# A decoder block on one core: the MLP's hidden-side S sums formed in the up projection, and the down projection's weight operands handled in units of 128x2048

## The chip, the cores and the metric

The kernel runs on one core of a Trainium2 chip. The metric is the device time of one execution in microseconds. The kernel before takes 1153.55 us in the median of three runs (1149.79, 1153.55 and 1154.32). Engines are named as in the profile: PE (TensorE matmul), PEld (its weight load), DVE (VectorE), ACT (ScalarE), POOL (GpSimd), and SP (SyncE, which only issues transfers). A line number Lnnn is one of the kernel before, unless the changed kernel is named.

## The reference

One layer of a decoder on 1024 tokens of 1024 channels (16 meta tokens are put in front and dropped again at the end). All data are float32.

```python
hn = rms_norm(h, norm_mix_w);  proj = hn @ w_in          # 3088 columns
mixed = concatenate([gla_branch(...), short_conv_branch(...)]) @ w_out
h = h + mixed
hn = rms_norm(h, norm_mlp_w)
h = h + square(relu(hn @ w_up)) @ w_down                 # 1024 -> 4096 -> 1024
out = rms_norm(h, norm_final_w)[:, N_META:]
```

The change touches only the last product pair, `square(relu(hn @ w_up)) @ w_down`. The three norm weights, w_up, w_down and the rest are inputs and may not be prepared outside the kernel.

## The kernel before

**Stages.** The first 390 us or so hold the input projection, the linear attention and the convolution. Then follow the output projection (tiles `mo`, `wo`), the up projection (16 groups of 256 hidden channels) and the down projection (four chunks of 1024 hidden channels, that is four groups each).

**Precision.** Each float32 operand is split into a high part, rounded to PE's float32r format by ACT (`split`, L76), and a low part, the difference, formed by DVE (L36). A product is three matmuls: high by high, high by low, low by high (`mm3`, L680 to L682).

**Seven products for eight.** From the up projection on, every product is a 2 x 2 block product in Winograd's form. With A the stationary side and B the moving one:

```
S1 = A21+A22, S2 = S1-A11, S3 = A11-A21, S4 = A12-S2
T1 = B12-B11, T2 = B22-T1, T3 = B22-B12, T4 = B21-T2
```

The seven products are called 1 (A11 B11), 2 (A12 B21), 5 (S1 T1), 6 (S2 T2), 7 (S3 T3), 3 (S4 B22) and 4 (A22 T4). Each has its own operands, and each of these is split.

**The up projection.** A is w_up, B the normalised input. A group's seven products are 12 matmuls each. POOL forms the four S sums of a group (tiles `S`, 128x512), ACT and DVE split the seven operands (`wh_u`, `wl_u`) about a group ahead of PE. `up_first` does products 1 and 2, the loop of phase 3 the other five. ACT takes the accumulators out of PSUM (L746, L886, L911), DVE and POOL add them up (L669), DVE squares the relu (L739), and SP stores four tiles a group (`put`, L740): the blocks of the hidden activation, token half by channel half. Two loads of w_up (`up_load`, L691, 512 KB each) stand among the stores in SP's queue. Their buffers are three, so a load also waits for operands to be split.

**The down projection.** A is the hidden activation, B is w_down. A product is 48 matmuls: four token tiles t, each with 12 matmuls into one PSUM bank. `a_load` (L937) and `b_load` (L943) fetch blocks of 128x2048 (1 MB) into rings of five slots a side, called `A...l` and `B...h` after the buffers that they reuse. `prep` makes the operands of a chunk's products in the order 1 2 5 6 7 3 4. POOL forms S1 to S4 (`each`, 16 operations of 128x512 a chunk), DVE forms T1 to T4 (also 16). `emit` splits A by token tile into pairs (`wh_d`, `wl_d`; eight pairs, so two products' worth) and B by row tile into a unit (`bo<chunk><product>h` and `l`, 128x2048; two units, so product n+1 reuses the unit of product n-1). After each token tile DVE adds the bank to the residual stream h (L669: `h<-da` for products 1, 6, 7, 4; `h<-db` for 2, 5, 3). Banks: four for `da`, four for `db`. At the end h is normalised and stored (L1004 to L1014).

**What sets the order.** Each engine executes its own list in order. A scheduler makes the lists from the order of the source when the program is built. The operands of a product are emitted ahead of the matmuls of the product before it (`ahead = next(st)`).

Of the kernel before, what the change touches and what calls it, by code (L numbers as in the profile page):

```python
# [30 lines left out]
def block_kernel(ctx: ExitStack, tc, x, meta, nmix, w_in, wgu, bgate, gnorm, conv_w,  # L31
# [42 lines left out]
    def split(src, hl, eng=None):  # L74
        """hi and lo parts of a float32 view into float32r views"""
        hi = nc.scalar.copy(hl[0], src)  # L76
        return hi, sub(eng or nc.vector, hl[1], src, hl[0].bitcast(F32))
# [40 lines left out]
    # ------------------------------------------------------------------ phase 1  # L118
    with ExitStack() as p1:
# [165 lines left out]
        with ExitStack() as p1b:  # L285
# [153 lines left out]
            def gla():  # L439
# [195 lines left out]
            # ---- output gate; the two groups' outputs, split, as units (half, group)  # L635
# [83 lines left out]
    def up_ready(g, ps):  # L719
        """operands ps of group g"""  # L720
# [13 lines left out]
    banks = {}  # L734

    def put(g, z, i, h):
        """squared relu of a tile of hidden channels, to DRAM"""
        c, k0 = divmod(2 * g, 8)
        nc.vector.scalar_tensor_tensor(z, z, 0.0, z, op0=ALU.max, op1=ALU.mult)  # L739
        nc.sync.dma_start(hidD[c][:, h * 4:(h + 1) * 4, k0 + i, :], z.rearrange("p (t c) -> p t c", c=P))  # L740

    def up_first(g, e1):
        """the products that need only the first half of the tokens"""
# [5 lines left out]
        put(g, e1, 0, 0)  # L749

    raws = {}
    with tc.tile_pool(name="p2", bufs=1, reuse_waits="tile") as p2:
# [107 lines left out]
        up_first(0, p2.tile([P, HALF], F32, tag="x1", name="e1_0", bufs=3))  # L860
# [3 lines left out]
        up_first(1, p2.tile([P, HALF], F32, tag="x1", name="e1_1", bufs=3))  # L864
        b_last()

    # ------------------------------------------------------------------ phase 3
    with tc.tile_pool(name="p3", bufs=1, reuse_waits="tile") as p3:
# [10 lines left out]
        for g in range(NG):  # L879
# [4 lines left out]
            def evac(ps, nm):  # L884
                e = p3.tile([P, HALF], F32, tag="e", name=f"{nm}_{g}", bufs=8)
# [3 lines left out]
            if g > 1:  # L889
                up_first(g, p3.tile([P, HALF], F32, tag="e", name=f"e1_{g}", bufs=8))  # L890
# [178 lines left out]
```

## Time and profile before

| | |
|---|---|
| median of three runs | 1153.55 us |
| span of the profiled execution | 1151.1 us (no other time is listed for it) |
| PE busy | 1090.6 us, 95% of the span |
| DVE busy | 773.0 us, 67% |
| ACT busy | 433.2 us, 38% |
| POOL busy | 347.0 us, 30% |
| DMA traffic | 107.52 MB |
| mean granted PE clock | 0.983 |

The busy shares are averages over stages with different limits, so they are read by stage: the view of windows gives busy times and the granted clock (PEclk) for a stretch, the view of a tile gives the first and last start of each kind of instruction, the view of waits says who waited for whom, and the timeline shows single instructions. A row of the timeline ends with `xN` where N instructions of one kind follow each other; its duration is then from the first start to the last end.

### The profile page before, as it was taken

Reading aid. Unit: us, or ns where it says so; the run is one execution under the profiler, and the core shown is the slowest. Engines: PE = TensorE matmul, PEld = TensorE weight load, DVE = VectorE, ACT = ScalarE, POOL = GpSimd, SP = SyncE. Lnnn points to the kernel's source line nnn. Section 1 sums busy time; section 2 is a strip of 40 time slices with the busy share of each in tenths; the row PEclk is TensorE's granted clock in tenths of the full one; section 3 lists DMA queues with packets and bytes.
Section 4 is the critical chain, followed back from the end, with each engine's and each line's share of the span. In section 5 each row is a group of like instructions: output and inputs, shape, how many; then the busy total and the mean of one; then the engine's idle time right before and its main releaser. Section 6 shows DMA issues by size and latency. Waiting matters only on the chain.

```text
span 1151.1 us, 13931 instructions
## 1 busy us (share of the span) xinstructions
PE 1090.6 (95%) x4954; PEld 892.4 (78%) x4954; DVE 773.0 (67%) x1210; ACT 433.2 (38%) x846; POOL 347.0 (30%) x396
## 2 busy tenths in 40 slices
PE   6999899999999999979999999999899799899897
PEld 4888687878788888758888888888678688687686
DVE  5421677866873525996555555655799988978976
ACT  5332543343423423434333333334244334334352
POOL 2300243423210001564424242420535406306303
PEclk9999999999999999989999999999999999899899
DMA  7221110111110524125342424237645063152003
GB/s 240 57 58 37 55 37 1 37 37 38 36 38 1 170 86 146 67 90 190 112 138 83 137 83 138 83 101 224 188 137 156 3 194 97 36 180 77 1 1 147
DMA packets 119575, 107.52 MB, mean 93 GB/s; under 512 B 7456, under 2 KB 99648, under 8 KB 119504
## 3 DMA queue, kind: packets, MB, share of 16 engines
q1 hardware_dynamic: 119504, 106.62, 29.7%
q8 instruction: 39, 0.64, 0.2%
q14 instruction: 32, 0.26, 0.1%
HBM read 81.44 MB, written 25.17 MB: 93 GB/s over the span
## 4 chain that ended last, share of the span: by engine, by line
PE 76%; DVE 15%; issue 3%; DMA 2%; POOL 2%; ACT 1%; SPq 1%; DVEq 0%; POOLq 0%; ACTq 0%
PE ua L681 5%; PE ua L682 5%; PE ua L680 5%; PE da L680 3%; PE da L681 3%; PE da L682 3%; PE db L680 3%; PE db L681 3%; PE db L682 3%; DVE wl_d L36 2%; PE uc L681 2%; PE uc L680 2%; PE uc L682 2%; PE mo L681 2%; PE mo L680 2%
## 5 line engine op out<-in xcount | busy, mean ns | idle before, releaser
L36 DVE TENSOR_TENSOR wl_u<-S,wh_u 128x512 fp32r<-128x512 f32 x64 | 68.9, 1079 | 88.1 <-ACT wh_u L76 88.1
L36 POOL TENSOR_TENSOR d<-bT 128x128 f32<-128x128 f32 x112 | 52.5, 490 | 126.4 <-DVE qtb L39 60.3
L669 DVE TENSOR_TENSOR h<-da,h 128x512 f32<-128x512 f32 x64 | 43.8, 686 | 23.8 <-PE da L682 23.8
L669 POOL TENSOR_TENSOR S<-wr_up,wr_up 128x512 f32<-128x512 f32 x16 | 21.0, 1311 | 125.1 <-DVE wl_u L36 116.1
L76 ACT CAST wh_u<-wr_up 128x512 fp32r<-128x512 f32 x48 | 29.8, 624 | 60.5 <-PE ua L681 48.1
L500 ACT ACTIVATE d<-d 128x256 f32<-128x256 f32 x56 | 23.4, 418 | 63.4 <-POOL d L36 60.2
L36 DVE TENSOR_TENSOR wl_u<-wr_up,wh_u 128x512 fp32r<-128x512 f32 x48 | 46.9, 979 | 0.0
L39 DVE TENSOR_TENSOR qtb<-qT,d 64x128 f32<-64x128 f32 x112 | 42.1, 376 | 2.7 <-ACT d L500 1.4
L669 DVE TENSOR_TENSOR h<-db,h 128x512 f32<-128x512 f32 x48 | 32.9, 688 | 11.8 <-PE db L682 11.8
L76 ACT CAST wh_u<-S 128x512 fp32r<-128x512 f32 x64 | 37.9, 622 | 0.6 <-POOL S L36 0.6
L39 DVE TENSOR_TENSOR kt<-kT,d 128x256 f32<-128x256 f32 x56 | 24.0, 441 | 18.6 <-ACT d L500 7.0
L669 DVE TENSOR_TENSOR xr<-mo,xr 128x512 f32<-128x512 f32 x16 | 11.0, 690 | 33.7 <-PE mo L682 29.7
L515 PEld LDWEIGHTS pa<-qtb,kt 128*128 128x128 f32 x224 | 29.7, 191 | 4.5 <-ACT abuf L525 1.2
L777 POOL TENSOR_SCALAR sq<-sq 128x1 f32<-128x1 f32 x8 | 1.5, 190 | 104.6 <-ACT j L775 104.6
L886 ACT COPY ev<-ua 128x512 f32<-128x512 f32 x16 | 9.4, 588 | 61.4 <-PE ua L682 61.4
L669 POOL TENSOR_TENSOR ew<-ew,e 128x512 f32<-128x512 f32 x16 | 21.9, 1366 | 34.6 <-ACT ew L886 33.2
L515 PE MATMUL pa<-qtb,kt 128*128 128x128 f32 x224 | 31.9, 279 | 0.3 <-DVE abuf L529 0.2
L681 PE MATMUL ua<-T3l,wh_u 128*128 128x512 f32 x64 | 26.0, 407 | 5.5 <-DVE T3l L36 5.5
L36 POOL TENSOR_TENSOR S<-wr_up 128x512 f32<-128x512 f32 x16 | 25.3, 1580 | 6.9 <-DVE wl_u L36 6.9
L669 DVE TENSOR_TENSOR e<-ub,e 128x512 f32<-128x512 f32 x16 | 11.0, 689 | 23.2 <-PE ub L682 10.8
L682 PE MATMUL ua<-B11h,wl_u 128*128 128x512 f32 x64 | 25.7, 402 | 0.5 <-DVE wl_u L36 0.5
L36 POOL TENSOR_TENSOR S<-S,wr_up 128x512 f32<-128x512 f32 x16 | 21.1, 1316 | 16.8 <-DVE wl_u L36 16.6
(777 smaller groups left out, 3721.8 us busy)
## 6 DMA issues: line engine op xcount, KB each, us to landing
wr_up<-in_w_up SPq DMA_DIRECT2D x32, 512.0 KB, 4.9
hidD<-e SPq DMA_DIRECT2D x32, 256.0 KB, 3.6
xt<-in_x SPq DMA_DIRECT2D x8, 512.0 KB, 3.5
wr_wo<-in_w_out SPq DMA_DIRECT2D x8, 512.0 KB, 3.7
xr<-in_x SPq DMA_DIRECT2D x16, 256.0 KB, 5.3
hD<-xr SPq DMA_DIRECT2D x16, 256.0 KB, 2.8
h<-hD SPq DMA_DIRECT2D x8, 512.0 KB, 5.5
hidD<-ew SPq DMA_DIRECT2D x16, 256.0 KB, 2.3
```

The costliest lines, as they stand in the source:

```text
L36: return eng.tensor_tensor(o, a, b, op=ALU.subtract)
L39: eng.tensor_tensor(o, a, b, op=ALU.mult)
L76: hi = nc.scalar.copy(hl[0], src)
L500: nc.scalar.activation(d, d, AF.Exp, scale=1.0 / 16)
L515: nc.tensor.matmul(pa[c][:, li % 2, 2 * p:2 * p + 2, :], kk[:, c * P:(c + 1) * P], qq[:, :, c * 64:(c + 1) * 64], start=True, stop=True)
L669: return eng.tensor_tensor(o, a, b, op=ALU.add)
L680: nc.tensor.matmul(ps, sh, xh, start=start and k == 0, stop=False, skip_group_check=not start)
L681: nc.tensor.matmul(ps, sh, xl, start=False, stop=False, skip_group_check=not start)
L682: nc.tensor.matmul(ps, sl, xh, start=False, stop=(k == n - 1), skip_group_check=not start)
L777: nc.gpsimd.tensor_scalar(sq, sq, 1.0 / D, EPS, op0=ALU.mult, op1=ALU.add)
L886: evacs.append(nc.scalar.copy(e, ps))
```

## The change

1. **S sums of the hidden side move from the down projection to the up projection.** There, after a group's tiles are squared, DVE forms S1, S3 (over the tile `ev`), S2 and S4 of the group's 128x512 tiles. Seven tiles a group are stored instead of four, each in its own DRAM block `hid<c>_<product>`; the block 21 alone (`ev` before S3) is no longer needed and not stored. In the down projection `a_load` fetches the finished operand of a product with one transfer, seven a chunk instead of four blocks in four transfers each, and POOL forms no sums any more.
2. **Layout.** A stored tile is 128x512 with 2048 contiguous bytes in each partition's row, where the row was cut into pieces of 128 columns before. With that, one K half of a chunk holds the first 128 channels of each of its four groups and the other half the second 128; `b_load` picks w_down's rows to match.
3. **Units.** T1 to T4 and the split of B are single operations of 128x2048 on DVE and ACT, where they were four of 128x512. The first two products of chunk 0 keep the fine split.
4. **Buffers.** The tiles `e` of the up projection go from 8 to 11 (`NE`), `e1` gets a tag of its own with two buffers, and `dynamic_dma_scratch_size=2048` leaves room for them. Comments and docstrings are dropped, which moves line numbers.

```diff
-    hidD = [dram.tile([P, 8, KT, P], F32, name=f"hidD{c}") for c in range(4)]
+    hidD = [{p: dram.tile([P, 4, HALF], F32, name=f"hid{c}_{p}") for p in "1256734"} for c in range(4)]
+    NE = 11
...
+    def store(g, p, z):
+        c, k = divmod(g, 4)
+        nc.sync.dma_start(hidD[c][p][:, k, :], z)
+
+    def put(g, z, p=None):
         nc.vector.scalar_tensor_tensor(z, z, 0.0, z, op0=ALU.max, op1=ALU.mult)
-        nc.sync.dma_start(hidD[c][:, h * 4:(h + 1) * 4, k0 + i, :], z.rearrange("p (t c) -> p t c", c=P))
+        if p:
+            store(g, p, z)
...
             plus(nc.gpsimd, ew, ew, e5)
-            put(g, ew, 1, 1)
+            put(g, ew, "4")
             up_prod(g, "3", pc, False)
             plus(nc.vector, ev, pc, ev)
-            put(g, ev, 0, 1)
+            put(g, ev)
+            s1, s2, s4 = (p3.tile([P, HALF], F32, tag="e", name=f"hs{i}_{g}", bufs=NE) for i in "124")
+            plus(nc.vector, s1, ev, ew)
+            store(g, "5", s1)
+            sub(nc.vector, ev, z11[g], ev)
+            store(g, "7", ev)
+            sub(nc.vector, s2, s1, z11.pop(g))
+            store(g, "6", s2)
             up_ready(g + 1, "3")
             up_prod(g, "4", pa, False)
...
-            put(g, e4, 1, 0)
+            put(g, e4, "2")
+            sub(nc.vector, s4, e4, s2)
+            store(g, "3", s4)
             up_ready(g + 1, "4")
...
-        def a_load(c, i, kk):
-            q = quad("A", f"{c}{i}{kk}")
-            for t in range(4):
-                nc.sync.dma_start(q[:, :, t * P:(t + 1) * P], hidD[c][:, i * 4 + t, kk * 4:(kk + 1) * 4, :])
+        def a_load(c, p):
+            q = quad("A", f"{c}{p}")
+            nc.sync.dma_start(q, hidD[c][p])
             return q
...
-            nc.sync.dma_start(q, w_down[r0:r0 + 512, j * HALF:(j + 1) * HALF].rearrange("(a p) m -> p a m", p=P))
+            w = w_down[c * 1024:(c + 1) * 1024, j * HALF:(j + 1) * HALF]
+            nc.sync.dma_start(q, w.rearrange("(g k p) m -> k p g m", k=2, p=P)[kk])
...
+                fine = c == 0 and n < 2
+                if not fine:
+                    split(b, u)
                 for t in range(4):
                     hl = pair(f"d{nm}{p}{t}", [P, 4, P])
                     split(a[:, :, t * P:(t + 1) * P], hl)
                     av.append(hl)
-                    split(b[:, t, :], (u[0][:, t, :], u[1][:, t, :]))
+                    if fine:
+                        split(b[:, t, :], (u[0][:, t, :], u[1][:, t, :]))
...
-            s1, t2 = quad("A", f"s{nm}"), quad("B", f"t{nm}")
-            each(nc.gpsimd, plus, s1, a21, a22)
-            each(nc.vector, sub, b11, b12, b11)          # T1
-            yield emit("5", s1, b11, 2)
-            each(nc.gpsimd, sub, a21, a11, a21)          # S3
-            each(nc.gpsimd, sub, a11, s1, a11)           # S2
-            each(nc.vector, sub, t2, b22, b11)           # T2
-            yield emit("6", a11, t2, 3)
+            t2 = quad("B", f"t{nm}")
+            sub(nc.vector, b11, b12, b11)
+            yield emit("5", a5, b11, 2)
+            a7 = a_load(c, "7")
+            sub(nc.vector, t2, b22, b11)
+            yield emit("6", a6, t2, 3)
...
```

Three places in the lists matter for the prediction. The first is DVE at the end of group 12 of the up projection and the start of group 13 (`e` holds the tiles of the activation, `ev` and `ew` two of them, `hs` the new sums, `wl_u` the next operands). Before:

```order
L36 TENSOR_TENSOR wl_u_4_6254<-wr_up_5963,wh_u_4_6253 128x512
L739 SCALAR_TENSOR_TENSOR ev_6173<-ev_6173 128x512
L36 TENSOR_TENSOR wl_u_1_6302<-wr_up_6109,wh_u_1_6301 128x512
L739 SCALAR_TENSOR_TENSOR e_12_6249<-e_12_6249 128x512
L36 TENSOR_TENSOR wl_u_2_6306<-wr_up_6111,wh_u_2_6305 128x512
```

Now:

```order
L36 TENSOR_TENSOR wl_u_4_6408<-wr_up_6097,wh_u_4_6407 128x512
L745 SCALAR_TENSOR_TENSOR ev_6317<-ev_6317 128x512
L669 TENSOR_TENSOR hs_12_6376<-ev_6317,ew_6353 128x512
L36 TENSOR_TENSOR ev_6317<-e_12_6257,ev_6317 128x512
L36 TENSOR_TENSOR hs_12_6377<-hs_12_6376,e_12_6257 128x512
L745 SCALAR_TENSOR_TENSOR e_12_6401<-e_12_6401 128x512
L36 TENSOR_TENSOR wl_u_1_6456<-wr_up_6253,wh_u_1_6455 128x512
L36 TENSOR_TENSOR hs_12_6378<-e_12_6401,hs_12_6377 128x512
L36 TENSOR_TENSOR wl_u_2_6460<-wr_up_6255,wh_u_2_6459 128x512
```

Four operations are added behind the squaring of `ev`: S1, S3 and S2 ahead of the squaring of e4 and of `wl_u_1`, and S4 between `wl_u_1` and `wl_u_2`.

The second is SP in the same group, stores and loads of w_up (the loads are those of group 15). Before:

```order
L740 DMA hidD_3419<-ew_6209 128x4x128
L691 DMA wr_up_6257<-in_w_up 128x4x256
L740 DMA hidD_3419<-ev_6173 128x4x128
L691 DMA wr_up_6259<-in_w_up 128x4x256
L740 DMA hidD_3419<-e_12_6249 128x4x128
```

Now:

```order
L741 DMA hid_4_3443<-ew_6353 128x512
L693 DMA wr_up_6411<-in_w_up 128x4x256
L741 DMA hid_5_3439<-hs_12_6376 128x512
L741 DMA hid_7_3441<-ev_6317 128x512
L741 DMA hid_6_3440<-hs_12_6377 128x512
L741 DMA hid_2_3438<-e_12_6401 128x512
L741 DMA hid_3_3442<-hs_12_6378 128x512
L693 DMA wr_up_6413<-in_w_up 128x4x256
```

The second load of w_up stood ahead of the store of e4; it now stands behind it and behind the store of S4, the last sum of the group.

The third is DVE in the down projection, chunk 1, at the end of product 1 and the start of product 2, where the operands of product 5 are made (`bo15l` is their B part, `wl_d<-As1l` before and `wl_d<-A15l` now their A parts; `B101h` becomes T3 and `B110h` T4). Before:

```order
L669 TENSOR_TENSOR h_4921<-da_7396,h_4921 128x512
L36 TENSOR_TENSOR wl_d_7449<-As1l,wh_d_7448 128x512
L36 TENSOR_TENSOR B101h<-B111h,B101h 128x512 x2
L669 TENSOR_TENSOR h_4923<-da_7410,h_4923 128x512
L36 TENSOR_TENSOR bo15l<-B100h,bo15h 128x512 x3
L36 TENSOR_TENSOR wl_d_7455<-As1l,wh_d_7454 128x512
L36 TENSOR_TENSOR bo15l<-B100h,bo15h 128x512
L669 TENSOR_TENSOR h_4917<-db_7460,h_4917 128x512
L36 TENSOR_TENSOR wl_d_7531<-A100l,wh_d_7530 128x512
L36 TENSOR_TENSOR B110h<-B110h,Bt1h 128x512
```

Now:

```order
L36 TENSOR_TENSOR B101h<-B111h,B101h 128x2048
L669 TENSOR_TENSOR h_4985<-da_7491,h_4985 128x512
L36 TENSOR_TENSOR wl_d_7534<-A15l,wh_d_7533 128x512
L669 TENSOR_TENSOR h_4987<-da_7505,h_4987 128x512
L36 TENSOR_TENSOR wl_d_7538<-A15l,wh_d_7537 128x512
L36 TENSOR_TENSOR B110h<-B110h,Bt1h 128x2048
L36 TENSOR_TENSOR bo15l<-B100h,bo15h 128x2048
L669 TENSOR_TENSOR h_4981<-db_7541,h_4981 128x512
```

Where four operations of 128x512 stood with additions to h between them, there is one of 128x2048. T4 (`B110h`) stood behind the first addition of product 2's banks (`h<-db`) before and stands ahead of `bo15l` now, and that addition waits behind both.

More of the change, by code (lines that the diff above doesn't have):

```diff
@@ L732, in up_prod, with up_first @@
             lambda k: (bu[p][0][:, k, :], bu[p][1][:, k, :]), 4, start)
-    banks = {}
-    def put(g, z, i, h):
-        c, k0 = divmod(2 * g, 8)
+    banks, z11 = {}, {}
+    def store(g, p, z):
+        c, k = divmod(g, 4)
+        nc.sync.dma_start(hidD[c][p][:, k, :], z)
+    def put(g, z, p=None):
         nc.vector.scalar_tensor_tensor(z, z, 0.0, z, op0=ALU.max, op1=ALU.mult)
-        nc.sync.dma_start(hidD[c][:, h * 4:(h + 1) * 4, k0 + i, :], z.rearrange("p (t c) -> p t c", c=P))
-    def up_first(g, e1):
+        if p:
+            store(g, p, z)
+    def up_first(g):
+        e1 = ps3.tile([P, HALF], F32, tag="e1", name=f"e1_{g}", bufs=2)
         pa, pb = banks[g] = bank("a", f"ua{g}"), bank("b", f"ub{g}")
@@ L748, in up_first @@
         plus(nc.vector, e1, pb, e1)
-        put(g, e1, 0, 0)
+        put(g, e1, "1")
+        z11[g] = e1
     raws = {}
@@ L859, in block_kernel @@
         raws[1] = up_load(1)
-        up_first(0, p2.tile([P, HALF], F32, tag="x1", name="e1_0", bufs=3))
+        up_first(0)
         up_ready(1, "12")
@@ L863, in block_kernel @@
         up_ready(0, ORDER[2:])
-        up_first(1, p2.tile([P, HALF], F32, tag="x1", name="e1_1", bufs=3))
+        up_first(1)
         b_last()
@@ L884, in evac @@
             def evac(ps, nm):
-                e = p3.tile([P, HALF], F32, tag="e", name=f"{nm}_{g}", bufs=8)
+                e = p3.tile([P, HALF], F32, tag="e", name=f"{nm}_{g}", bufs=NE)
                 evacs.append(nc.scalar.copy(e, ps))
@@ L889, in block_kernel @@
             if g > 1:
-                up_first(g, p3.tile([P, HALF], F32, tag="e", name=f"e1_{g}", bufs=8))
+                up_first(g)
             pa, pb = banks.pop(g)
@@ L903, in block_kernel @@
             plus(nc.gpsimd, ew, ew, e5)
-            put(g, ew, 1, 1)
+            put(g, ew, "4")
             up_prod(g, "3", pc, False)
             plus(nc.vector, ev, pc, ev)
-            put(g, ev, 0, 1)
+            put(g, ev)
[6 more added lines that the diff above has]
+            store(g, "6", s2)
             up_ready(g + 1, "3")
             up_prod(g, "4", pa, False)
-            e4 = p3.tile([P, HALF], F32, tag="e", name=f"e4_{g}", bufs=8)
+            e4 = p3.tile([P, HALF], F32, tag="e", name=f"e4_{g}", bufs=NE)
             nc.scalar.activation(e4, pa, AF.Relu)
-            put(g, e4, 1, 0)
+            put(g, e4, "2")
+            sub(nc.vector, s4, e4, s2)
+            store(g, "3", s4)
             up_ready(g + 1, "4")
@@ L941, in b_load @@
             q = quad("B", f"{c}{kk}{j}")
-            r0 = c * 1024 + kk * 512
-            nc.sync.dma_start(q, w_down[r0:r0 + 512, j * HALF:(j + 1) * HALF].rearrange("(a p) m -> p a m", p=P))
+            w = w_down[c * 1024:(c + 1) * 1024, j * HALF:(j + 1) * HALF]
+            nc.sync.dma_start(q, w.rearrange("(g k p) m -> k p g m", k=2, p=P)[kk])
             return q
@@ L958, in emit @@
                     av.append(hl)
-                    split(b[:, t, :], (u[0][:, t, :], u[1][:, t, :]))
+                    if fine:
+                        split(b[:, t, :], (u[0][:, t, :], u[1][:, t, :]))
                 return av, u
-            def each(eng, f, o, a, b):
-                for t in range(4):
-                    f(eng, o[:, t, :], a[:, t, :], b[:, t, :])
-            a11, b11 = a_load(c, 0, 0), b_load(c, 0, 0)
-            yield emit("1", a11, b11, 0)
-            a12, b21 = a_load(c, 0, 1), b_load(c, 1, 0)
+            a1, b11 = a_load(c, "1"), b_load(c, 0, 0)
+            yield emit("1", a1, b11, 0)
+            a2, b21 = a_load(c, "2"), b_load(c, 1, 0)
             b12 = b_load(c, 0, 1)
-            a21, a22 = a_load(c, 1, 0), a_load(c, 1, 1)
+            a5 = a_load(c, "5")
+            b22 = b_load(c, 1, 1)
             if c == 0:
                 load_h(p4, range(6, 8))
-            b22 = b_load(c, 1, 1)
-            yield emit("2", a12, b21, 1)
-            s1, t2 = quad("A", f"s{nm}"), quad("B", f"t{nm}")
-            each(nc.gpsimd, plus, s1, a21, a22)
-            each(nc.vector, sub, b11, b12, b11)
-            yield emit("5", s1, b11, 2)
-            each(nc.gpsimd, sub, a21, a11, a21)
-            each(nc.gpsimd, sub, a11, s1, a11)
-            each(nc.vector, sub, t2, b22, b11)
-            yield emit("6", a11, t2, 3)
-            each(nc.vector, sub, b12, b22, b12)
-            yield emit("7", a21, b12, 4)
-            each(nc.gpsimd, sub, a12, a12, a11)
-            each(nc.vector, sub, b21, b21, t2)
-            yield emit("3", a12, b22, 5)
-            yield emit("4", a22, b21, 6)
+            a6 = a_load(c, "6")
+            yield emit("2", a2, b21, 1)
+            t2 = quad("B", f"t{nm}")
[4 more added lines that the diff above has]
+            yield emit("6", a6, t2, 3)
+            a3 = a_load(c, "3")
+            sub(nc.vector, b12, b22, b12)
+            yield emit("7", a7, b12, 4)
+            a4 = a_load(c, "4")
+            sub(nc.vector, b21, b21, t2)
+            yield emit("3", a3, b22, 5)
+            yield emit("4", a4, b21, 6)
         def down_prod(ps, av, u, t, start):
@@ L1055 @@
               "w_up": (D, DFF), "w_down": (DFF, D), "norm_final_w": (1, D)}
-    nc = bacc.Bacc("TRN2", target_bir_lowering=False, num_devices=1)
+    nc = bacc.Bacc("TRN2", target_bir_lowering=False, num_devices=1, dynamic_dma_scratch_size=2048)
     arrays, args = {}, []
```

## The prediction

> **What bounds the kernel now.** I read the windows by stage first (busy us and count by engine, granted clock, DMA share), then the rows of the down projection's tiles (ns min/median/max, first and last start in us), then the waits from 804 us on (total us, times, longest).
>
> ```profile
> 525.00:800.00 275.00, 274.89 (x1213) 227.38 (x1212) 155.47 (x192) 98.20 (x177) 89.69 (x66) 1.00 0.41 121
> ...
> 804.10:879.10 75.00, 67.55 (x287) 54.84 (x286) 65.52 (x91) 27.34 (x49) 25.85 (x18) 0.95 0.61 191
> ...
> 965.10:1050.00 84.90, 80.76 (x341) 65.89 (x340) 75.00 (x102) 32.83 (x59) 28.70 (x17) 0.96 0.32 100
> ...
> L680 PE MATMUL da<-bo01h,wh_d x16: 389/389/389, 804.1 to 814.3; 128*128 128x512 f32 x16
> ...
> L680 PE MATMUL db<-bo02h,wh_d x16: 389/389/389, 815.0 to 825.2; 128*128 128x512 f32 x16
> ...
> L680 PE MATMUL db<-bo05h,wh_d x16: 389/394/767, 831.6 to 845.1; 128*128 128x512 f32 x16
> ...
> L680 PE MATMUL da<-bo11h,wh_d x16: 389/389/497, 890.6 to 903.8; 128*128 128x512 f32 x16
> ...
> L680 PE MATMUL da<-bo21h,wh_d x16: 389/389/628, 974.1 to 988.4; 128*128 128x512 f32 x16
> ...
> L680 PE MATMUL da<-bo26h,wh_d x16: 389/389/389, 1014.7 to 1024.9; 128*128 128x512 f32 x16
> ...
> L680 PE MATMUL da<-bo31h,wh_d x16: 389/389/499, 1058.2 to 1071.1; 128*128 128x512 f32 x16
> ...
> L680 PE MATMUL da<-bo34h,wh_d x16: 389/389/389, 1132.6 to 1142.8; 128*128 128x512 f32 x16
> ...
> PE db L680 <- DVE h L669: 14.9, 5, 5.5
> ...
> PE da L680 <- DVE h L669: 7.3, 3, 2.7
> ```
>
> In the up projection PE is full at the full clock and DVE has 57% (155.47 of 275 us). In the down projection PE has gaps, its clock sinks behind them (matmuls of 389 ns reach 628 and 767), and DVE is busy 87 to 88%. Products 6, 7, 3 and 4 of chunk 2 run without a gap: 1014.7 to 1058.2 is 43.5 us, so a product takes 10.875 us and 28 take 304.5. The stage runs from 804.1 to 1132.6 + 10.9 = 1143.5, that is 339.4 us: 34.9 us are lost. The chunks' starts share it out: 86.5, 83.5, 84.1 and 85.3 us against 76.1 each. The last two rows name DVE's additions to h, which free the banks.
>
> Why is DVE late? The timeline of DVE and POOL around chunk 2's start:
>
> ```profile
> 942.87 2.49 DVE L36 TENSOR_TENSOR bo13l<-B111h,bo13h 128x512 fp32r<-128x512 f32 x4
> ...
> 965.27 6.89 DVE L36 TENSOR_TENSOR bo21l<-B200h,bo21h 128x512 fp32r<-128x512 f32 x4
> ...
> 966.47 6.85 POOL L36 TENSOR_TENSOR A210l<-A200l,A210l 128x512 f32<-128x512 f32 x4
> ...
> 972.08 0.68 DVE L669 TENSOR_TENSOR h<-da,h 128x512 f32<-128x512 f32 x1
> ```
>
> Four subtractions of one kind take 2.49 us with POOL idle (0.60 from one to the next, the last 0.69) and 6.89 with POOL at its S sums (1.73 each). The addition that reads PSUM keeps 0.68. So POOL's 16 sums a chunk, about 27 us, hold DVE to a third of its pace on SBUF operands: in 27 us it does 16 operations where 45 would fit, some 17 us of DVE lost a chunk.
>
> **The change, part by part.**
>
> *S sums off POOL.* A chunk's DVE list is then 28 additions, 28 A splits, 7 B units and 4 T units. At 0.60 for the small ones and 2.4 a unit this is 33.6 + 26.4 = 60 us, under PE's 76.1. The dearest product (5, 6, 7 and 4 have a T each) takes 2.4 + 2.4 + 8 x 0.60 = 9.6 of 10.9 us. PE becomes the bound: up to -34.9 us.
>
> *Units of 128x2048.* None is in the trace.
>
> ```profile
> L39 DVE TENSOR_TENSOR kt<-kT,d 128x256 f32<-128x256 f32 x56 | 24.0, 441 | 18.6 <-ACT d L500 7.0
> ...
> L669 DVE TENSOR_TENSOR h<-da,h 128x512 f32<-128x512 f32 x64 | 43.8, 686 | 23.8 <-PE da L682 23.8
> ...
> 880.26 2.18 ACT L76 CAST bo11h<-B100h 128x512 fp32r<-128x512 f32 x4
> ```
>
> From 128x256 to 128x512 DVE adds 245 ns, so 2048 columns give 686 + 6 x 245 = 2.2 us; four small ones give 2.5. The other end is the paired price, 6.9. I take 2.4, nearest to the row with POOL idle, and 2.2 for ACT. [...]
>
> A unit delays what is queued behind it. At product 5 the list (third order excerpt) has, once product 2 begins: addition of product 1's last tile, last A split, T4, `bo15l`: 0.7 + 0.6 + 2.4 + 2.4 = 6.1 us. ACT's cast needs the unit that product 1 has just left, 2.2 us plus the last A cast, and is done before. The bank that product 5 needs is freed by the next addition, at 6.7 us of 10.9. Cover 4.2 us; no stall.
>
> *Four sums and three stores more per up group.* DVE and POOL in one group of the up projection, then SP:
>
> ```profile
> 661.70 1.28 POOL L669 TENSOR_TENSOR S<-wr_up,wr_up 128x512 f32<-128x512 f32 x1 [9.32 <-DVE wl_u L36]
> ...
> 670.13 1.29 POOL L36 TENSOR_TENSOR S<-wr_up,S 128x512 f32<-128x512 f32 x1 [0.69 <-DVE wl_u L36]
> ...
> 680.74 1.28 POOL L669 TENSOR_TENSOR S<-wr_up,wr_up 128x512 f32<-128x512 f32 x1 [9.32 <-DVE wl_u L36]
> ...
> 683.48 1.29 POOL L36 TENSOR_TENSOR S<-S,wr_up 128x512 f32<-128x512 f32 x1 [1.45 <-DVE wl_u L36]
> ...
> 684.88 1.29 POOL L669 TENSOR_TENSOR ew<-ew,e 128x512 f32<-128x512 f32 x1
> ...
> 687.25 1.78 DVE L36 TENSOR_TENSOR wl_u<-S,wh_u 128x512 fp32r<-128x512 f32 x1
> ...
> 689.55 1.47 DVE L36 TENSOR_TENSOR wl_u<-wr_up,wh_u 128x512 fp32r<-128x512 f32 x1
> ...
> 671.90 0.68 DVE L739 SCALAR_TENSOR_TENSOR ev<-ev 128x512 f32<-128x512 f32 x1
> ...
> 676.12 0.69 DVE L669 TENSOR_TENSOR e<-ub,e 128x512 f32<-128x512 f32 x1 [1.66 <-DMA hidD<-ev]
> ...
> 667.67 0.62 ACT L76 CAST wh_u<-wr_up 128x512 fp32r<-128x512 f32 x1 [0.87 <-PE uc L681]
> ...
> 679.92 0.69 DVE L36 TENSOR_TENSOR wl_u<-S,wh_u 128x512 fp32r<-128x512 f32 x1 [2.38 <-ACT wh_u L76]
> ...
> 673.25 0.37 SPq L691 DMA_DIRECT2D wr_up<-in_w_up  x1
> ...
> wr_up<-in_w_up SPq DMA_DIRECT2D x32, 512.0 KB, 4.9
> ```
>
> A group lasts 19.04 us (661.70 to 680.74). The sums follow `ev`'s squaring at 671.90, when POOL's last sum of the group is over (670.13 + 1.29): 4 x 0.60 = 2.4 us, into idle times of 1.66 and 2.38. [...] If all four met POOL, the rows price them at 1.73, 6.9 us; even then DVE has 0.57 x 19.04 = 10.8 and 6.9, 17.7 of 19.04. Nor does PE wait for DVE here: ACT's casts wait for PE to leave one of the eight pairs of operand buffers (row of 667.67), so an operand is begun seven products of 2.72 us before its use, 19 us, of which I take 14 as cover after its making. Cost 0; without that cover, 2.4 us a group.
>
> SP's second w_up load moves from 673.25 to behind S4: 671.90 plus seven operations of 0.60 (squaring, S1, S3, S2, squaring, `wl_u_1`, S4) is 676.1, the store's issue 0.6, so 676.7. It lands 4.9 later, at 681.6, a microsecond after POOL's first sum would start (680.74), while the second (683.48) still waits for DVE. Cost 0.
>
> *Hand-over at 804.* Timeline rows of SP, ACT and POOL there, loads with their time to landing (last number, us), and a row of the chain of waits:
>
> ```profile
> 792.57 0.36 SPq L740 DMA_DIRECT2D hidD<-e  x1
> ...
> 797.37 0.62 ACT L76 CAST bo01h<-B000h 128x512 fp32r<-128x512 f32 x1 [2.43 <-DMA B000h<-in_w_down]
> ...
> 801.12 1.56 POOL L669 TENSOR_TENSOR ew<-ew,e 128x512 f32<-128x512 f32 x1 [19.74 <-ACT ew L886]
> ...
> 808.07 0.36 SPq L740 DMA_DIRECT2D hidD<-e  x1
> ...
> B100h<-in_w_down SPq DMA_DIRECT2D x1, 1024.0 KB, 4.9
> ...
> B001h<-in_w_down SPq DMA_DIRECT2D x1, 1024.0 KB, 8.6
> ...
> 818.97 5.04 POOL As0l L669 x4
> ```
>
> The load of B000 now stands behind the store at 792.57. Issued at 793.0 and landed after 4.9 to 8.6 us (the rows of B100h and B001h), it gives ACT its first cast at 798 to 801.6, against 797.37 now. Two casts, the copy of ew, POOL's addition (1.56), then DVE's squaring, the addition of ev and the last of four low pieces: 801.6 + 1.2 + 0.6 + 1.6 + 3 x 0.6 is 806.8 at the late end. PE needs that piece nine matmuls after 804.1, at 806.1. The stall is 0 to 2 us; I take 1. Product 5 lost 5.7 us (831.6 against 825.9) to the loads of A010 and A011, then POOL. Now A05 comes ready-made, issued behind the last store, which moves from 808.07 to about 810 (the sums). With at most 8.6 us it lands by 819; four casts and splits take 3 us, so 822 is the latest for 825.9. Covered by 3 us; if it lands later, product 5 waits as long. The chain's last row is POOL's sum that goes.
>
> *DMA traffic.* Three stores of 256 KB more in 16 groups and three blocks of 1 MB more in four chunks, 12.6 MB each, on 107.52 MB, at shares of 0.41 (up) and 0.32 to 0.61 (down): hidden, except as a rival below. The tail behind the last matmul, 1151.1 - 1143.5 = 7.6 us, stays.
>
> **The sum.** 804.1 + 1 + 304.5 + 7.6 = 1117.2 against a span of 1151.1, -33.9. The median of the runs, 1153.55, is 2.45 above that span: 1119.7, so 1120.
>
> **The rivals.**
> *The hand-over stays starved (0.10).* In place of POOL's sums, A05, A06 and their B loads crowd behind the stores of group 15, and a wait for DMA takes the place of the one removed: chunk 0 keeps nearly its loss of 10.4, so 1120 + 9 = 1129. For: the DMA share of 0.61 there, the highest. Against: no POOL step behind the load, and one transfer in place of four.
> *The units are slow (0.07).* At the paired 6.9 us the addition at product 5 comes at 0.7 + 0.6 + 6.9 + 6.9 + 0.6 = 15.7, 4.8 late, four times: 1139. It decides from 4.5 us a unit on. For: no operation of that size is in the trace. Against: POOL has no sums left there.
> *The cause is another (0.05).* DVE was held by its own order and not by POOL, so the additions to h stay as late as they are: within 5 us of 1153. For: the additions stand behind operand work in DVE's list, before and after. Against: 2.49 and 6.89 us for one code.
> *Slower: the up projection becomes a ring (0.04).* The second w_up load now waits for S4, and the next S4 for it: store 0.6, load 4.9, POOL's two sums and ew behind them 3.9, DVE's squaring 0.6, two low parts of 1.78 and 1.47, two short operations 1.2 and six more up to S4 3.6, a circle of 18.1 us against 19.04. If the load, behind three more stores, takes p us over 5.9, groups last p longer, some 13 times, less the 14 us that PE is ahead. It eats the gain of 33.9 from p = 3.7, a load of 9.6 us; at 10.6 it is 1120 + 13 x 4.7 - 14 = 1167. For: B001 took 8.6 in a crowd. Against: w_up's loads take 4.9 there.
>
> **How the numbers follow.** The forecast has 0.74, with its own range 1114 to 1126 (the stall 0 to 2, runs 0.4% apart). To leave out no more than 2 in 10 and hold the slow hand-over and the low end of slow units, the range is 1114 to 1136. Faster by over 0.5%: 0.74 + 0.10 + 0.07 = 0.91; within 0.5%, about what a measurement of this kernel can tell: 0.05; slower: 0.04.
>
> **What would show it.** Right: products 10.9 us apart from 804 on, PEclk 1.00 in the down windows, units of about 2.4 us, DVE idle before h on PE, and the group still 19.04. Wrong: waits of PE on `h<-db` at product 5 (units), on A05 or A06 (hand-over), groups over 19.04 with `S` waiting for w_up (ring).

## The result and the profile after

The changed kernel takes 1116.96 us (median; 1116.01 to 1117.64) against 1153.4 of the kernel before (median of four runs), a ratio of 0.9691 with a 95% interval of 0.9673 to 0.9709: faster by 36 us, where 1120 with a range of 1114 to 1136 was predicted. The profiled execution took 1117.64 us, its span is 1115.9.

The windows of the changed kernel (the stretch in us, its length, busy us and count of PE, weight load, DVE, ACT and POOL, then the granted clock, the DMA share and GB/s):

```profile
525.00:800.00 275.00, 275.00 (x1215) 227.54 (x1214) 193.25 (x249) 96.81 (x175) 91.72 (x66) 1.00 0.48 162
804.10:879.10 75.00, 75.00 (x333) 62.10 (x332) 65.53 (x80) 29.95 (x39) 0.00 (x0) 1.00 0.75 280
880.00:955.00 75.00, 75.00 (x332) 62.12 (x331) 58.13 (x66) 30.10 (x35) 0.00 (x0) 1.00 0.44 155
955.00:1030.00 75.00, 75.00 (x332) 62.11 (x331) 58.13 (x67) 29.94 (x35) 0.00 (x0) 1.00 0.44 154
475.00:525.00 50.00, 40.08 (x166) 31.45 (x165) 47.22 (x53) 22.54 (x43) 32.18 (x24) 0.90 0.33 111
```

From 525 us on PE is full at the full clock, in the down projection too, where POOL has nothing to do and DVE 58.1 of 75 us (65.5 in chunk 0). Between 390 us and the end of the down projection PE's only gaps now lie at 475 to 525, the start of the up projection, which the change does not touch. The first matmuls of products (ns min/median/max, first and last start):

```profile
L682 PE MATMUL da<-bo01h,wh_d x16: 389/389/389, 803.8 to 814.0; 128*128 128x512 f32 x16
L682 PE MATMUL da<-bo11h,wh_d x16: 389/389/389, 880.0 to 890.2; 128*128 128x512 f32 x16
L682 PE MATMUL da<-bo21h,wh_d x16: 389/389/389, 956.2 to 966.4; 128*128 128x512 f32 x16
L682 PE MATMUL da<-bo31h,wh_d x16: 389/389/389, 1032.3 to 1042.5; 128*128 128x512 f32 x16
L682 PE MATMUL da<-bo34h,wh_d x16: 389/389/389, 1097.6 to 1107.8; 128*128 128x512 f32 x16
```

The chunks are 76.2, 76.2 and 76.1 us apart, where 86.5, 83.5 and 84.1 stood before, and none of these matmuls is stretched. The waits of the down projection have turned round: none of PE is left, and DVE waits for PE (total us, times, longest):

```profile
DVE h L669 <- PE da L684: 21.3, 18, 1.4
DVE h L669 <- PE db L684: 21.0, 17, 1.4
```

Two units, from the view of one line of code (ns min/median/max, start):

```profile
L36 DVE TENSOR_TENSOR Bt1h<-B111h,B100h x1: 2281/2281/2281, 879.6 to 879.6; 128x2048 f32<-128x2048 f32 x1
L36 DVE TENSOR_TENSOR bo12l<-B110h,bo12h x1: 2292/2292/2292, 882.4 to 882.4; 128x2048 fp32r<-128x2048 f32 x1
```

One thing is new, and it is not on PE's path. In the up projection POOL now waits, in ten groups, for the second w_up load, which stands on SP behind the store of S4. A row of the waits from 525 to 804 us:

```profile
POOL S L669 <- DMA wr_up<-in_w_up: 95.5, 10, 11.1
```

POOL's timeline:

```profile
664.66 1.29 POOL L669 TENSOR_TENSOR S<-wr_up,wr_up 128x512 f32<-128x512 f32 x1 [10.99 <-DMA wr_up<-in_w_up]
...
683.97 1.30 POOL L669 TENSOR_TENSOR S<-wr_up,wr_up 128x512 f32<-128x512 f32 x1 [11.12 <-DMA wr_up<-in_w_up]
```

SP's timeline, with the store of S4 at 677.88 and second loads of w_up:

```profile
545.31 0.38 SPq L693 DMA_DIRECT2D wr_up<-in_w_up  x1
...
677.88 0.32 SPq L741 DMA_DIRECT2D hid<-hs  x1
678.30 0.54 SPq L693 DMA_DIRECT2D wr_up<-in_w_up  x1
...
697.87 0.39 SPq L693 DMA_DIRECT2D wr_up<-in_w_up  x1
...
754.60 0.41 SPq L693 DMA_DIRECT2D wr_up<-in_w_up  x1
```

These two groups of POOL are 19.31 us apart, but from the load at 545.31 to the one at 754.60, eleven groups on, it is 19.03 each, PE's own group of 19.04. So the ring of the slower rival is there and keeps pace, but with no room to be seen: the nine turns that begin with a load for which POOL waits take 18.29 us (the one from 545.31) to 19.57 (the one from 678.30), and 18.99 in the mean.

### The profile page after: what moved, and what is told of

It reads as the page before. It is cut to its first block, busy times and chain, and to the rows that moved or that the text cites. A ratio compares the mean times of both kernels' runs of the same rounds, so it can differ in the third digit from the quotient of the medians.

```text
span 1115.9 us, 13780 instructions
## 1 busy us (share of the span) xinstructions
PE 1079.5 (97%) x4954; PEld 887.2 (79%) x4954; DVE 757.0 (68%) x1148; ACT 425.7 (38%) x768; POOL 243.8 (22%) x332
## 3 DMA queue, kind: packets, MB, share of 16 engines
q1 hardware_dynamic: 72080, 131.79, 34.7%
## 4 chain that ended last, share of the span: by engine, by line
PE 88%; DVE 7%; issue 1%; POOL 1%; ACT 1%; DMA 1%; SPq 0%; DVEq 0%; POOLq 0%; ACTq 0%
PE da L683 5%; PE da L684 5%; PE da L682 5%; PE ua L683 5%; PE ua L684 5%; PE ua L682 5%; PE db L684 4%; PE db L683 4%; PE db L682 4%; PE uc L682 3%; PE uc L683 3%; PE uc L684 3%; PE mo L683 2%; PE mo L684 2%; PE mo L682 2%; PE pa L515 2%
## 5 line engine op out<-in xcount | busy, mean ns | idle before, releaser
L36 DVE TENSOR_TENSOR wl_u<-S,wh_u 128x512 fp32r<-128x512 f32 x64 | 58.8, 924 | 61.3 <-ACT wh_u L76 61.3
L1034 POOL TENSOR_SCALAR fs<-fs 128x1 f32<-128x1 f32 x8 | 4.9, 617 | 284.5 <-ACT fj L1022 284.4
L669 POOL TENSOR_TENSOR ew<-ew,e 128x512 f32<-128x512 f32 x16 | 26.2, 1636 | 39.7 <-ACT ew L895 39.7
L745 DVE SCALAR_TENSOR_TENSOR ew<-ew 128x512 f32<-128x512 f32 x16 | 23.8, 1490 | 14.2 <-POOL ew L669 14.2
L784 ACT ACTIVATE j<-xr 128x512 bf16<-128x512 f32 x16 | 10.1, 634 | 41.6 <-DVE xr L669 41.6
L684 PE MATMUL ua<-T3h,wl_u 128*128 128x512 f32 x64 | 25.9, 404 | 0.0
```

The lines of the kernel that those rows point to most:

```text
L36: return eng.tensor_tensor(o, a, b, op=ALU.subtract)
L669: return eng.tensor_tensor(o, a, b, op=ALU.add)
L684: nc.tensor.matmul(ps, sl, xh, start=False, stop=(k == n - 1), skip_group_check=not start)
L784: nc.scalar.activation(junk, ht, AF.Square, accum_out=sq)
```

## Experiments

The theory: POOL's operations that read SBUF, 16 of them a chunk, hold DVE's operations with SBUF operands (1.73 us from one to the next in place of 0.60 in the kernel before), and that was the whole loss in the down projection. There are three rivals: the units made the gain, by fewer instructions; DVE waited for POOL's sums as operands; or any work of POOL holds DVE, reading or not. All runs are compared with the kernel before on the same chip; times are medians, and ratios go to the kernel before.

### The sums alone, the units alone

The changed kernel with every B split and T in 128x512:

```diff
-                fine = c == 0 and n < 2
+                fine = True
...
-            sub(nc.vector, b11, b12, b11)
+            each(nc.vector, sub, b11, b12, b11)
...
```

> The changed kernel, but with every B split and every T of the down projection in four pieces of 128x512, as before the change. Theory (the sums on POOL were all of the loss): DVE's list in a chunk is 28 additions + 28 A pieces + 28 B pieces + 16 T pieces = 100 operations of 0.60 us, 60 us, as much as with the units, under PE's 76.1: 1117, at most 2 us beside the changed kernel, chunks 76.1 apart. Rival (the larger units carry part of the gain, by fewer instructions): 1122 to 1130, with gaps of PE ahead of products 5 to 4.

1117.09 us, ratio 0.9685 (0.9671 to 0.9699): the same time as with the units. DVE has 60.32 of 75 us in the windows from 880 on, where the units make it 58.13. The other half, the kernel before with units, POOL's sums left in place:

```diff
+                fine = c == 0 and n < 2
+                if not fine:
+                    split(b, u)
...
-            each(nc.vector, sub, b11, b12, b11)          # T1
+            sub(nc.vector, b11, b12, b11)          # T1
...
```

> The kernel before, with the B splits and the T in units of 128x2048 and the S sums left on POOL in the down projection. Theory: a unit that meets POOL's sums takes about 6.9 us (four times 1.73), so DVE loses as much as before, and one unit delays the additions to h more than a piece does: 1150 to 1160. Rival (the units are what gained): 1140 or less, DVE busy in the down projection below 80%.

1149.68 us, ratio 0.9967 (0.9954 to 0.9980). That is on the theory's side, though 3.6 us better than before where no gain was expected. Its DVE timeline at the start of chunk 2 shows units that are held for less long than expected:

```profile
965.53 2.46 DVE L36 TENSOR_TENSOR bo21l<-B200h,bo21h 128x2048 fp32r<-128x2048 f32 x1 [0.84 <-ACT bo21h L76]
967.91 0.68 DVE L669 TENSOR_TENSOR h<-da,h 128x512 f32<-128x512 f32 x1
968.51 1.18 DVE L36 TENSOR_TENSOR wl_d<-A201l,wh_d 128x512 fp32r<-128x512 f32 x1
...
971.32 3.38 DVE L36 TENSOR_TENSOR B200h<-B201h,B200h 128x2048 f32<-128x2048 f32 x1
```

A unit beside POOL takes 3.38 us, not 6.9: that is 1.1 us over the 2.28 of a unit with POOL idle, and not 1.1 at each quarter.

### The sums to DVE, with no other change

```diff
-            each(nc.gpsimd, plus, s1, a21, a22)
+            each(nc.vector, plus, s1, a21, a22)
...
-            each(nc.gpsimd, sub, a21, a11, a21)          # S3
-            each(nc.gpsimd, sub, a11, s1, a11)           # S2
+            each(nc.vector, sub, a21, a11, a21)          # S3
+            each(nc.vector, sub, a11, s1, a11)           # S2
```

(S4 likewise.)

> The kernel before, with the four S sums of a chunk of the down projection on DVE in place of POOL, and nothing else: no unit, no store and no load more. DVE's list grows from 100 to 116 operations of a chunk. Theory (POOL's operations, and not the amount of work, held DVE): 116 x 0.60 = 70 us, still under PE's 76.1, so most of the gain comes: 1119 to 1130, DVE busy about 93% there, operations 0.60 apart at the chunk's start in place of 1.73. Rival (the cause is the order on DVE, the loads or the amount of work): 1145 or more.

1120.38 us, ratio 0.9711 (0.9695 to 0.9727). DVE was given 16 operations a chunk more, and 33 of the 36 us came. Its windows:

```profile
804.10:879.10 75.00, 72.23 (x316) 58.78 (x315) 69.40 (x116) 30.40 (x56) 0.00 (x0) 1.00 0.62 190
880.00:955.00 75.00, 75.00 (x332) 62.10 (x332) 69.83 (x116) 31.37 (x56) 0.00 (x0) 1.00 0.37 113
```

DVE at 69.83 of 75 us still keeps up. The 3.4 us to the changed kernel lie in chunk 0, where PE has 72.23 of 75. A row of the waits there:

```profile
DVE As0l L669 <- DMA A011l<-hidD: 5.0, 1, 5.0
```

The sum S1 waits on DVE for a load, and holds what is queued behind it. In the changed kernel the block comes ready-made and chunk 0 has no gap.

### POOL operations whose result nobody needs

Reads, in the changed kernel:

```diff
...
             sub(nc.vector, t2, b22, b11)
+            for n in range(16):
+                plus(nc.gpsimd, idle, a5[:, n % 4, :], a6[:, n % 4, :])
```

> The changed kernel, with 16 additions of 128x512 a chunk on POOL that read two loaded blocks (A05 and A06 of the chunk) and write a tile that nothing reads: no operation of another engine waits for them. Theory (POOL's operations with SBUF operands hold DVE, whoever needs their result): DVE's operations are 1.73 us apart and a unit takes about 6.9 us while they run, some 17 us of DVE lost a chunk on a list of 60: 1130 to 1152. Rival (DVE was late because it waited for the sums as operands): 1116 to 1119, as without them.

1136.36 us, ratio 0.9848 (0.9834 to 0.9863): the loss comes back without any data dependence, but only half of it. POOL's timeline (16 additions in each row):

```profile
825.96 33.89 POOL L669 TENSOR_TENSOR idle<-A05l,A06l 128x512 f32<-128x512 f32 x16 [24.41 <-DMA A06l<-hid]
877.73 34.60 POOL L669 TENSOR_TENSOR idle<-A15l,A16l 128x512 f32<-128x512 f32 x16 [17.89 <-DMA A16l<-hid]
948.77 33.03 POOL L669 TENSOR_TENSOR idle<-A25l,A26l 128x512 f32<-128x512 f32 x16 [36.44 <-DMA A26l<-hid]
```

The first matmuls of chunks 1, 2 and 3:

```profile
L682 PE MATMUL da<-bo11h,wh_d x16: 389/389/390, 891.4 to 901.6; 128*128 128x512 f32 x16
L682 PE MATMUL da<-bo21h,wh_d x16: 389/389/389, 974.9 to 985.1; 128*128 128x512 f32 x16
L682 PE MATMUL da<-bo31h,wh_d x16: 389/389/389, 1051.2 to 1061.4; 128*128 128x512 f32 x16
```

Chunk 1, whose reads begin 14 us ahead of it, takes 83.5 us; chunk 2, whose reads begin 26 us ahead, 76.3. So either the place of the stretch decides, or the other half of the loss before was waiting for the sums. To tell these apart the same 16 reads were tied to the chunk's first unit:

```diff
...
+            first = emit("1", a1, b11, 0)
+            yield first
...
+            plus(nc.gpsimd, idle, first[1][1][:, 0, :].bitcast(F32), a5[:, 0, :])
+            for n in range(15):
+                plus(nc.gpsimd, idle, a5[:, n % 4, :], a6[:, n % 4, :])
             sub(nc.vector, b11, b12, b11)
```

> As the run e4_pool_reads (16 additions a chunk on POOL whose result nobody reads), but the first of them reads the low part of the chunk's first B unit, so that the stretch begins just before the chunk's first product, as POOL's S sums did in the kernel before (960.6 us for a chunk that begins at 974), and not when A06 lands (948.8 for a chunk that begins at about 975, mostly under the chunk before it). Theory (the loss is DVE's lost time in the stretch in which the T and the B units fall due; in e4_pool_reads chunks 2 and 3 escaped by their early start): all four chunks lose, 1142 to 1155. Rival (the other half of the loss came from waiting for the sums themselves as operands): 1134 to 1138 as there.

1157.99 us, ratio 1.0043 (1.0028 to 1.0058): 3 us over what was expected, and slower than the kernel before, with all else as in the changed one. The first matmuls of chunks 1 and 2:

```profile
L682 PE MATMUL da<-bo11h,wh_d x16: 389/389/390, 892.8 to 903.0; 128*128 128x512 f32 x16
L682 PE MATMUL da<-bo21h,wh_d x16: 389/389/390, 977.4 to 987.6; 128*128 128x512 f32 x16
```

Chunks 0 to 2 take 89.0, 84.6 and 84.9 us. DVE's timeline at the start of chunk 2 (977.4):

```profile
971.76 1.47 DVE L36 TENSOR_TENSOR wl_d<-A22l,wh_d 128x512 fp32r<-128x512 f32 x1
973.14 0.68 DVE L669 TENSOR_TENSOR h<-da,h 128x512 f32<-128x512 f32 x1
973.75 1.18 DVE L36 TENSOR_TENSOR wl_d<-A22l,wh_d 128x512 fp32r<-128x512 f32 x1
974.85 3.38 DVE L36 TENSOR_TENSOR B200h<-B201h,B200h 128x2048 f32<-128x2048 f32 x1
```

And POOL's:

```profile
972.75 35.20 POOL L669 TENSOR_TENSOR idle<-A25l,A26l 128x512 f32<-128x512 f32 x15
```

So the place decides: under the first products of a chunk, where T1, T2 and the first units fall due, the stretch costs 8 to 13 us a chunk (84.6 to 89.0 against 76.1); under the last products of the chunk before, where DVE waits for PE anyway (17 times on `da`, up to 1.4 us, in the first of the two runs), it costs next to nothing (76.3). A wait for the sums themselves need not be assumed. Last, POOL as busy with writes alone (64 settings to zero in place of the 16 additions):

```diff
...
+            plus(nc.gpsimd, idle[:, 0:P], a5[:, 0, 0:P], a6[:, 0, 0:P])
+            for n in range(64):
+                nc.gpsimd.memset(idle, 0.0)
```

> The changed kernel, with POOL kept busy in each chunk of the down projection by 64 settings of a 128x512 tile to zero (about 0.53 us each, 34 us a chunk, as long as the 16 additions that cost 19 us a run took together), begun behind one addition of 128x128 that reads A05 and A06. They read nothing. Theory (the loss comes from POOL's reading of SBUF operands): DVE keeps 0.60 us from one small operation to the next and 2.3 a unit, and the time is that of the changed kernel, 1116 to 1119. Rival (any work of POOL on SBUF, writing too, holds DVE): 1130 to 1145, as with the additions.

1117.36 us, ratio 0.9698 (0.9682 to 0.9714): no loss at all. POOL's group of the settings (count, busy us, mean ns, idle before):

```profile
L1002 POOL MEMSET idle<- 128x512 f32 x256 | 135.1, 528 | 14.7
```

DVE's timeline while they run:

```profile
887.37 2.28 DVE L36 TENSOR_TENSOR B101h<-B111h,B101h 128x2048 f32<-128x2048 f32 x1
889.57 0.68 DVE L669 TENSOR_TENSOR h<-da,h 128x512 f32<-128x512 f32 x1
890.17 0.68 DVE L36 TENSOR_TENSOR wl_d<-A15l,wh_d 128x512 fp32r<-128x512 f32 x1
```

135 us of POOL in the down projection cost nothing where it reads nothing (1117.36 us against 1116.96); the additions, 33 to 35 us a chunk, cost 19.4 and 41.0 us a run. An operation of POOL that reads a single operand was not tried.

### How near the ring in the up projection is

S2 is formed five times (the same result), and the second w_up load is pinned behind S4's store, where it stands in the changed kernel:

```diff
-            sub(nc.vector, s2, s1, z11.pop(g))
+            z = z11.pop(g)
+            for _ in range(5):
+                sub(nc.vector, s2, s1, z)
...
+        if s4_store:
+            queue_after(ins, s4_store[-1])
...
```

> The changed kernel, with the sum S2 of the up projection formed five times in place of once (4 more DVE operations of 128x512 a group, same result), ahead of S4, and the second w_up load held behind S4's store as it is in the changed kernel. Theory (the ring load, POOL's sums, ew, DVE, S4, store, load turns in 19.3 us and PE's lead hides it): 4 x 0.60 = 2.4 us more a turn, more where POOL meets them; 21.7 or more against PE's 19.04, 2.7 x 13 less the 14 us of lead is 21 us: 1130 to 1150, PE waiting for wl_u late in the up projection. Rival (there is no ring, only DVE work, of which DVE has 193 of 275 us and room for 2.4 of 19): 1116 to 1119.

1152.10 us, ratio 0.9989 (0.9976 to 1.0001): four small operations a group eat the whole gain, and the time is 2 us over the theory's upper end. The same four without the pin, where SP's list has the load ahead of the stores of S2 and S4:

> The same four more DVE operations a group, but with the second w_up load two places earlier on SP's queue, ahead of the stores of S2 and S4 (so it waits for the store of product 4's square, behind one S2 only). Theory (the ring and not DVE's work sets the period): the extra operations lie outside the circle; 1116 to 1120, groups at 19.0 to 19.4 us. Rival (DVE's work): as slow as with the load held behind S4.

1118.94 us, ratio 0.9710 (0.9693 to 0.9727). DVE had the same work in the same order; the place of one load on a queue makes 33 us. Half the lengthening, with the pin (S2 three times):

> As the run e6_ring_long, but with S2 formed three times (two more DVE operations a group). That run was 35.1 us slower than the changed kernel, 13 turns of 21.72 - 19.03 = 2.69 us, with nothing taken off for a lead of PE. Theory (the circle of the changed kernel is 21.72 - 2.4 = 19.3 us, as long as PE's group, and PE has no lead to spend): a turn of 20.5, 13 x 1.5 = 19 us: 1132 to 1138. Rival (a lead of 14 us, and something else in that run): 1117 to 1123.

1127.16 us, ratio 0.9778 (0.9757 to 0.9798): between the two expectations, neither right. SP's timeline with two operations more, two loads eleven turns apart:

```profile
548.56 0.38 SPq L695 DMA_DIRECT2D wr_up<-in_w_up  x1
...
765.70 0.38 SPq L695 DMA_DIRECT2D wr_up<-in_w_up  x1
```

Its first product of the down projection:

```profile
L682 PE MATMUL da<-bo01h,wh_d x16: 389/389/389, 813.0 to 823.2; 128*128 128x512 f32 x16
```

A wait of ACT in it:

```profile
ACT wh_d L76 <- DMA A01l<-hid: 12.7, 1, 12.7
```

With four operations more, SP's timeline:

```profile
551.07 0.38 SPq L695 DMA_DIRECT2D wr_up<-in_w_up  x1
...
789.97 0.38 SPq L695 DMA_DIRECT2D wr_up<-in_w_up  x1
```

And its first product:

```profile
L682 PE MATMUL da<-bo01h,wh_d x16: 389/389/389, 838.5 to 848.7; 128*128 128x512 f32 x16
```

A turn is 19.74 and 21.72 us. Over PE's 19.03 that is 0.71 and 2.69, 13 times 9.2 and 35.0; the first product of the down projection is 9.2 and 34.7 us later than at 803.8. So nothing is taken off for PE's lead: with two more, PE loses 4.15 of the 275 us up to 800, and the rest at the hand-over, where ACT waits for A01, whose load stands on the same queue behind the ring's stores (issued at 795.30 against 788.79). That 13 turns give the lateness to 0.3 us is in part chance: A01 and B000 are issued 6.5 and 6.4 us later with two operations more, 32.1 and 33.4 with four, and with two ACT's first cast of B000, which waits for the load, starts 8.5 us after its issue (807.2), where it started 6.7 after it (798.95).

Two operations of 0.60 off 19.74 would leave 18.5 for the changed kernel's own circle, half a microsecond under the group. This is an estimate, and its own turns (18.99 in the mean) do not show that room. What fills it was not tried; in the group from 659.13 POOL's addition of ew takes 1.74 us beside a low part on DVE that comes at PE's pace (wl_u at 666.35, 1.51 us), while with two operations more the low parts are done before, and DVE stands idle for 5.97 us ahead of ew's squaring (at 655.74). The second pair of operations costs 1.98 a turn and not 1.2. In DVE's list of that kernel S4 has moved behind the addition of the next group's product 2, so three operations and not two are new ahead of S4; at 0.60 each that is 1.8 us of the 1.98.

### The same step at the start of the up projection

At 475 to 525 us PE has 40.08 of 50, DVE 47.22, and POOL's sums run beside DVE. T3, T4 and the S sums of group 1 go to DVE:

```diff
-                sub(nc.gpsimd, b11f[o], t2f[o], b11f[o])
+                sub(nc.vector, b11f[o], t2f[o], b11f[o])
...
-                sub(nc.gpsimd, t2f[o], f32(b[0]), t2f[o])
-                plus(nc.gpsimd, t2f[o], t2f[o], f32(b[1]))
+                sub(nc.vector, t2f[o], f32(b[0]), t2f[o])
+                plus(nc.vector, t2f[o], t2f[o], f32(b[1]))
...
```

(The S sums of group 1 likewise.)

> The changed kernel, with the same step taken at the start of the up projection: the sums T3 and T4 of the normalised input (12 operations of 128x512) and the S sums of group 1 (4) on DVE in place of POOL. Between 475 and 525 us PE has 40.1 of 50 us and DVE 47.2. Theory (there too POOL's reads hold DVE: single DVE operations take 1.4 to 1.8 us in place of 0.68): 16 x 0.60 = 9.6 us come to DVE, and some 15 meetings at 1.1 go; 3 to 8 us of PE's 9.9 come back: 1109 to 1114. Rival (DVE has only more to do there): 1117 to 1124.

1117.57 us, ratio 0.9701 (0.9685 to 0.9717): no gain. On DVE the theory held, since T3's low parts are done at 505.4 in place of 512.7, but the time did not follow. In the changed kernel PE's largest wait there was for these low parts:

```profile
PE ua L683 <- DVE T3l L36: 5.5, 1, 5.5
```

ACT's timeline of the new run tells what took the wait's place:

```profile
510.89 0.62 ACT L76 CAST T4h<-t 128x512 fp32r<-128x512 f32 x1 [1.79 <-DVE t L669]
511.41 0.58 ACT L896 COPY ev<-ua 128x512 f32<-128x512 f32 x1
```

And PE's largest wait in the new run:

```profile
PE ua L682 <- ACT ev L896: 11.1, 1, 11.1
```

In the changed kernel this copy came at 505.91, before T3 was ready; now it stands behind the last T4 cast. Group 0's product 6 and its copy were therefore put ahead of T3 and T4, into a tile of its own:

```diff
...
+        ev0 = ps3.tile([P, HALF], F32, tag="ev0", name="ev0")
+        up_prod(0, "6", banks[0][0], False)
+        evacs.append(nc.scalar.copy(ev0, banks[0][0]))
         b_last()
...
```

> The start of the up projection on DVE as in the run e8_dve_start (T3, T4 and the S sums of group 1 off POOL), and in addition the evacuation of group 0's product 6 (ev) into a tile of its own, copied ahead of the casts of T3 and T4 on ACT. In e8_dve_start DVE had T3's low parts ready at 505.4 us in place of 512.7, yet PE waited until 511.9 for ev, which stood on ACT behind the last T4 cast (510.9). Theory (only that place on ACT kept the gain away): PE goes on at about 505.5, waits some 1 us more for T4, and 4 to 6 us come back: 1111 to 1114. Rival (DVE has too much to do there in any order): 1116 to 1118.

1111.97 us (1110.75 to 1112.69), ratio 0.9647 (0.9629 to 0.9665): 5 us under the changed kernel, the fastest of all. Its waits of PE there:

```profile
PE ua L682 <- ACT T3h L76: 3.0, 1, 3.0
PE ua L684 <- DVE wl_u L36: 1.6, 1, 1.6
PE ua L683 <- DVE T3l L36: 0.7, 1, 0.7
```

## Why the prediction held, and where it did not

**The bound and its cause: right.** The excess of 34.9 us is gone as a whole, PE is the bound, and the sums carry it: without them on POOL the units are worth nothing (1117.09 against 1116.96), with them 3.6 us. The 1.73 us against 0.60 came from POOL's reading and from no wait for an operand, which the reads that nobody needs (1136.36 and 1157.99 us), and the writes that cost nothing (1117.36), show.

**The sum.** First matmul of the down projection 804.1 predicted, 803.8 measured; stall 1, measured 0 (the range of 0 to 2 was wider than its own working, which at the late end gives 806.8 - 806.1 = 0.7); 28 products 304.5, measured 304.7 (803.8 to 1097.6 + 10.9); tail 7.6, measured 7.4. The span came out at 1115.9 against 1117.2. Of the 3 us between 1120 and 1117, 1.4 are the distance from median to span, 1.1 here and 2.45 in the execution before.

**Units.** 2.28 to 2.29 us against 2.4 taken. The upper bound of 6.9 was wrong in its working: it let a unit meet POOL four times. Beside POOL it takes 3.38 (in the run with the units alone). So the rival of slow units, at 1139, had a price that nothing here reaches; at 3.4 us two units at product 5 come 2 us later than at 2.4, inside the cover of 4.2. DVE's list, 60 us by the sum, is 58.13 x 76.1 / 75 = 59.0.

**Four sums and three stores a group: cost 0 was right, its reasons only in part.** The load was put at 676.7 and its landing at 681.6, with POOL's second sum as the slack. It is issued at 678.30 and POOL's first sum waits for it until 683.97. That costs nothing because the circle keeps up with the group of 19.04, but nearer than the rival's sum of 18.1 says: where the load sets the pace, it takes 18.99 in the mean. The step that failed is the cover of 14 us "that PE is ahead": 13 turns of 0.71 and of 2.69 us make the down projection start 9.2 and 34.7 us later, with nothing taken off, since the hand-over takes its loads from the ring's queue and gives the lead back. The slower rival was therefore nearer than its formula said: it eats the gain at 2.7 us over the group, as the run with four operations more shows, where the formula with the lead asked for 3.7.

**Hand-over.** B000, behind a store, landed in time, as predicted (6.7 us after its issue); A05, issued at 810.82 where about 810 was predicted, took 7.2 us (at most 8.6 was assumed), and product 5 began at 825.6. The crowd of the first rival did come (B010 took 10.7 us, A06 12.2, A04 17.0), so that the 8.6 held for A05 was luck; the slower loads were needed later. The share of DMA rose from 0.61 to 0.75 in chunk 0 and PE did not feel it.

## What to carry to other kernels

Where DVE is the late engine, look first at what POOL reads at that time: 16 small additions a chunk that POOL "took off" DVE here cost DVE more (about 16 x 1.1 us, an estimate from 1.73 and 0.60) than doing them itself (16 x 0.60), and they cost most where DVE's work falls due (8 to 13 us a chunk), not where it waits (0.2). An operation moved off one engine frees time only when the next engine's order lets it through (1117.57 us at the start of the up projection, and 1111.97 with the copy moved), so read the list behind each releaser before costing the gain. A load queued behind a store that depends on an earlier load is a ring: add up its circle, and do not count a lead as cover when the next stage draws from the same queue.

## What the runs showed of the hardware that was not expected

A DVE operation with two SBUF operands took up to 1.1 us longer beside POOL's additions, at both sizes seen here: 1.73 us in place of 0.60 (128x512, from one to the next) and 3.38 in place of 2.28 (128x2048). That the larger one loses no more than the smaller was not expected. The 1.1 us are near the 1.29 of one POOL addition alone; that it is a wait for one such addition is an estimate, which no view shows. By it, a unit would be bounded by its own 2.28 and one POOL addition of 1.29, about 3.6 us, and not by 6.9. POOL's additions lengthen in turn: beside DVE's work they take 2.1 to 2.3 us in the mean (33.03 for 16, 35.20 for 15). POOL's writes did not lengthen DVE's operations: with 256 settings to zero of 0.53 us each, DVE stayed at 0.68 and 2.28.
